# Turning the score maxima of an attention layer: four products with the identity on TensorE, or a split on GpSimd and squares of 32 turned on VectorE

## The chip, the cores and the metric

The kernel runs on one core of a Trainium2 chip. The metric is the device time of one launch in microseconds (us). TensorE (PE in the profile) multiplies matrices, VectorE (DVE) and ScalarE (ACT) do elementwise work, GpSimd (POOL) is a third elementwise engine, and SyncE (SP) issues the transfers. Each engine takes its instructions in the order in which the program lists them, and an instruction that waits holds up everything behind it on its engine.

## The reference

One layer of a hybrid transformer: 2048 rows of width 1024, a context of 256 rows, a bidirectional retention with 4 heads, attention with 8 query heads on 2 key heads of width 64, and an MLP with squared ReLU. The change lies in the attention:

```
def _dense_attention(q, k, v):
    s = jnp.einsum('bqkgd,bskd->bkgqs', q, k).astype(jnp.float32) * ATT_SCALE
    p = jax.nn.softmax(s, axis=-1).astype(v.dtype)
    return jnp.einsum('bkgqs,bskd->bqkgd', p, v)
...
    k_all = jnp.concatenate([k_ctx, k_lat], axis=1)
    v_all = jnp.concatenate([v_ctx, v_lat], axis=1)
```

Every query sees all 2304 keys. The softmax needs a shift near the greatest score of each query, or its exponentials overflow.

## The kernel before

**Groups.** The 2048 queries are 16 tiles of 128 rows; a tile with one of the two key heads is a group, so there are 32 groups, numbered 0 to 31, of 4 heads x 128 queries. The 2304 keys are 18 tiles of 128. A group goes through two passes over them.

**First pass: maxima.** `piece` (L177, L181) multiplies the queries of one head with 512 keys into one of two PSUM banks called `mp`; `maximum` (L190) reduces that bank on VectorE into a column of `nm`. There are 18 such pairs for a group. `least` (L196) then reduces the 20 columns to the negated maximum of each query and head, and writes it twice, into columns 64 and 96 of a tile `mt` of 128x4x128 that is zero elsewhere and holds a constant in column 80.

**The turn.** The maxima lie down the partitions, one for each query, and the second pass wants them along the free dimension. `turn` (L201) transposes `mt` by four products with the identity on TensorE into an `mp` bank. `rows` (L204, ScalarE) copies rows 64 to 127 of that bank, divided by `ROW` = 8192, as float16 into `qr[64:, 1]`. `rows2` (L208, VectorE) writes the remainder of that rounding into rows 96 to 127.

**Second pass: scores.** `scores` makes a score tile of 128 keys x 512 (4 heads x 128 queries) with two products into one of two banks `st`: L214 with `qr[:, 0]`, L215 with `qr[:, 1]`, whose lower rows meet the rows of `unit` in `ks2` (`ROW` in its rows 0, 16 and 32) and so subtract the maximum inside the product. `exp` (L220, ScalarE) turns `st` into `p`; `cast` (L224, ScalarE) makes the float16 part `phi`; `low` makes the remainder `plo`, on GpSimd for five of nine pairs of key tiles (L231) and on VectorE for the others (L233); `values` (L247, L249) multiplies both parts with the values.

**Order.** All engines' orders are written out by hand: `on(k, phase, ...)` puts a call into step k, and the phases of a step run in a fixed list. Group n begins its first pass at step 18n and its second at step 18n + 22, so the first pass of one group lies beside the second of the one before. In the same steps run the retention (products `okw`, L1633; decays `oqf` and `oqb`, L1657; the normalisation of its output, whose root L1561 and factor `mr` L1695 on GpSimd feed four ScalarE instructions L1701), the output projection (L1837 to L1839) and, in the later groups, differences of `h` (L1929) and their float16 parts (L72, L73). Before the attention come the input products, after it the MLP (from about 1475 us).

Of the kernel before, what the change touches and what calls it, by code (L numbers as in the profile page):

```python
# [11 lines left out]
F32 = mybir.dt.float32  # L12
F32R = mybir.dt.float32r
F16 = mybir.dt.float16
BF16 = mybir.dt.bfloat16
I32 = mybir.dt.int32
AF = mybir.ActivationFunctionType
ALU = mybir.AluOpType
AX = mybir.AxisListType
# [3 lines left out]
P = 128  # L23
# [6 lines left out]
NK = NT + NC  # L30
H = 4
CH = 128
HD = 64
# [3 lines left out]
PSHIFT = 8  # L37

ROW = 8192.0
# [17 lines left out]
def layer_kernel(ctx: ExitStack, tc: tile.TileContext, a: dict, out: bass.AP):  # L57
    nc = tc.nc
# [5 lines left out]
    ident = const.tile([P, P], F32, name="ident")  # L64
# [70 lines left out]
    kp = keep.enter_context(tc.tile_pool(name="kp", bufs=1, reuse_waits="tile"))  # L135
# [6 lines left out]
    early = kp.tile([P, NK * (VW + 1)], F32, name="early", tag="wv")  # L142
# [6 lines left out]
    class Group:  # L149
# [7 lines left out]
        def load(self):  # L157
            pool, tag = (mq, "mb") if self.n % 4 < 2 else (qp, "qr")
            self.qr = pool.tile([P, 2, 4, P], F16, name="qr", tag=tag, bufs=2)
            q = self.qr.rearrange("p x (j e) t -> p x j e t", e=2)  # L160
            for e in range(2):
                src = aq_d[self.t][64 * e : 64 * e + 64, :, 2 * self.g : 2 * self.g + 2]
                nc.sync.dma_start(q[:64, :, :, e], src)
                nc.sync.dma_start(q[64:, 0, :, e], src[:, 0])

        def minima(self, pool):
            if pool is None:
# [21 lines left out]
                src, dst = m.rearrange("p (e k) -> p e k", e=2), self.nm[:, h, :, 4]  # L189
            nc.vector.tensor_reduce(dst, src, axis=AX.X, op=ALU.max, negate=True)  # L190

        def least(self, mt):
            self.mt = mt
            nm = self.nm.rearrange("p a b c -> p (a b) c")
            for c in (64, 96):
                nc.vector.tensor_reduce(mt[:, :, c], nm, axis=AX.X, op=ALU.min)  # L196

        def turn(self, pool=None, tag="mp"):
            self.m = (pool or psS).tile([P, 4, P], F32, name="mp", tag=tag)
            for h in range(4):  # L200
                nc.tensor.transpose(self.m[:, h], self.mt[:, h], ident)  # L201

        def rows(self):
            nc.scalar.activation(self.qr[64:, 1], self.m[64:], AF.Copy, scale=1 / ROW)  # L204

        def rows2(self):
            lo = self.qr[96:, 1]
            nc.vector.scalar_tensor_tensor(lo, self.m[96:], 1 / ROW, lo, op0=ALU.mult, op1=ALU.subtract)  # L208

        def scores(self, kt):  # L210
            ps = self.s[kt] = psS.tile([P, 512], F32, name="st", tag="st")
# [62 lines left out]
    with ExitStack() as st, tc.manual_schedule():  # L274
# [3 lines left out]
        wp = st.enter_context(tc.tile_pool(name="wp", bufs=12, reuse_waits="tile"))  # L278
        sg = st.enter_context(tc.tile_pool(name="sg", bufs=3, reuse_waits="tile"))
        op = st.enter_context(tc.tile_pool(name="op", bufs=2, reuse_waits="tile"))  # L280
# [4 lines left out]
        psO = st.enter_context(tc.tile_pool(name="psO", bufs=5, space=PSUM, reuse_waits="tile"))  # L285
# [25 lines left out]
        def do(s, part, fn, *args):  # L311
            steps.setdefault((s, part), []).append((fn, args))
# [897 lines left out]
        for (g, col), w in weights.items():  # L1210
            s = first[g, col]
# [3 lines left out]
            for j in range(w.n):  # L1215
                f, h = s - 5 + j, s - 3 + j if j < 2 else s - 1
                if (g, col) == (0, C_AQ):
                    f, h = s - 7 + j, s - 4 + j
                if (g, col) == (1, C_RQ):
                    f, h = s - 9 + j, (s - 6, s - 5, s - 2, s - 2)[j]  # L1220
                f, h = f - early_by, h - early_by
# [3 lines left out]
        for n, (col, s) in enumerate(((C_RK, 5), (C_AKV, 6), (C_AQ, 12), (C_RQ, 16), (C_RV, 18), (C_RG, 26))):  # L1225
            w = weights[0, col]
# [47 lines left out]
        s = first[1, C_RG]  # L1274
# [18 lines left out]
            do(s + 7 + i, "vec", next_g.maximum, i)  # L1293

        def first_mt():
            one_g.mt0 = wp.tile([P, 4, P], F32, name="mt", tag="w")
            nc.gpsimd.memset(one_g.mt0, 0.0)
            nc.gpsimd.memset(one_g.mt0[:, :, 80], PSHIFT * math.log(2.0) * HD**0.5)

        do(s + 4, "pool", first_mt)  # L1300
        do(s + 7, "vec", lambda: one_g.least(one_g.mt0))
        do(s + 8, "turn", one_g.turn, psO, "pso")
        do(s + 9, "turned", one_g.rows)
        do(s + 9, "low", one_g.rows2)

        def start():

# [217 lines left out]
    for g in range(2):  # L1525
        nc.sync.dma_start(ks2[:64, g], ks[:64, g])
        nc.sync.dma_start(ks2[64:, g], a["unit"])
    mts = [vp.tile([P, 4, P], F32, name=f"mt{i}") for i in range(2)]
    for mt in mts:
        nc.gpsimd.memset(mt, 0.0)  # L1530

        nc.gpsimd.memset(mt[:, :, 80], PSHIFT * math.log(2.0) * HD**0.5)

    def bank(i, shape=(P, 4, P)):
        return psX.tile(list(shape), F32, name=f"bank{i}", tag=f"bank{i}")
# [3 lines left out]
    def on(k, phase, fn, *args):  # L1539
        events.setdefault((k, phase), []).append((fn, args))  # L1540
# [28 lines left out]
    def attention():  # L1569
        for n, g in enumerate(groups):  # L1570
            k = NK * n
            if n > 0:
                if n > 1:
                    on(k - 14, "dma", g.load)
                    on(k - 1, "late", g.minima, sm)
                for i in range(AHEAD1 if n == 1 else 0, NK):
                    on(k + i, "piece", g.piece, i)
                    on(k + i + 1, "maximum", g.maximum, i)
                on(k + NK, "chain", g.least, mts[n % 2])
                on(k + NK + 1, "piece", g.turn)  # L1580
                on(k + NK + 2, "cast", g.rows)
                on(k + NK + 3, "early", g.rows2)
            k += LAG
            for i in range(NK):
                on(k + i, "scores", g.scores, i)
                on(k + i + 1, "exp", g.exp, i)
            for j in range(NK // 2):
                on(k + 2 * j + 3, "cast", g.cast, j)
                if j in POOL_PAIRS:
                    on(k + 2 * j + 4, "low", g.low, j)  # L1590
                else:
                    for i in range(2):
                        on(k + 2 * j + 4 + i, "low", g.low, j, i)
                on(k + 2 * j + 7, "values", g.values, j)
            k += NK + 6
            on(k, "cast", g.evacuate)
            on(k + 1, "chain", g.invert)
            on(k + 1, "late", g.combine, ats)
        return NK * len(groups) + LAG + 9
# [826 lines left out]
def _constants():  # L2426
    f = np.float32
    t = np.arange(SEQ, dtype=f)

    def freqs(n):  # L2430
        return (np.float32(10000.0) ** (-np.arange(n, dtype=f) / f(n))).astype(f)

    ang = (t[:, None] * freqs(64)).astype(f)
    c, s = np.cos(ang).astype(f), np.sin(ang).astype(f)
    ret = np.stack([np.concatenate([c, c], 1), np.concatenate([-s, s], 1)], 1)
    row = np.repeat(np.arange(SEQ // 64, dtype=f), 64)
    col = np.tile(np.arange(64, dtype=f), SEQ // 64)
    af = freqs(16)
    ang = np.concatenate([row[:, None] * af, col[:, None] * af], 1).astype(f)
    c, s = np.cos(ang).astype(f), np.sin(ang).astype(f)  # L2440
    att = np.stack([np.concatenate([c, c], 1), np.concatenate([-s, s], 1)], 1)
    j, i = np.meshgrid(np.arange(P), np.arange(P), indexing="ij")
    one = np.ones((P, P))
    rel = np.stack([np.maximum(i - j, 0), np.maximum(j - i, 0), one * (i + 1), one * (P - i)], 1).astype(f)
    pos = np.stack([P - 1 - np.arange(P), np.arange(P)], 1).astype(f)
    unit = np.zeros((64, NK * P), np.float16)
    unit[[0, 16, 32]] = ROW
    return {"ret_cs": ret, "att_cs": att, "rel": rel, "pos": pos, "unit": unit}


# [33 lines left out]
```

## Time and profile before

| | |
|---|---|
| median of 3 runs | 2664.66 us (2662.99 to 2667.97) |
| the profiled execution | 2665.0 us, span of its instructions 2663.2 us |
| busy: PE, DVE, ACT, POOL | 98%, 76%, 57%, 65% of the span |
| granted TensorE clock | 0.997 of full speed |
| first and last transpose of a `turn` on TensorE | 589.9 and 1443.0 us |

A row of the timeline gives start, duration, engine, line, operation, result and operands, and in brackets the idle time before it with what ended it. Rows of the groups end with the count, the busy time in us, the mean duration in ns, and the idle time before. TensorE overlaps its products, so the time that one occupies is read from start to start. Engine spans on POOL are rough.

### The profile page before, as it was taken

Reading aid. Unit: us, or ns where it says so; the run is one execution under the profiler, and the core shown is the slowest. Engines: PE = TensorE matmul, PEld = TensorE weight load, DVE = VectorE, ACT = ScalarE, POOL = GpSimd, SP = SyncE. Lnnn points to the kernel's source line nnn. Section 1 sums busy time; section 2 is a strip of 40 time slices with the busy share of each in tenths; the row PEclk is TensorE's granted clock in tenths of the full one; section 3 lists DMA queues with packets and bytes.
Section 4 is the critical chain, followed back from the end, with each engine's and each line's share of the span. In section 5 each row is a group of like instructions: output and inputs, shape, how many; then the busy total and the mean of one; then the engine's idle time right before and its main releaser. Section 6 shows DMA issues by size and latency. Waiting matters only on the chain.

```text
span 2663.2 us, 45648 instructions
## 1 busy us (share of the span) xinstructions
PE 2615.4 (98%) x16745; PEld 1466.2 (55%) x16745; DVE 2028.8 (76%) x3035; ACT 1526.2 (57%) x2576; POOL 1741.0 (65%) x1355
## 2 busy tenths in 40 slices
PE   8999999998999999999999999999999999999998
PEld 5875555545666666666666444444444444444443
DVE  5778798667888888888887597888886656656686
ACT  3856343426877788888888476666665322222243
POOL 3635566545666668787887696677663666666686
PEclk9999999999999999999999999999999999999999
DMA  6776899736112123233422664677684757475453
GB/s 230 272 247 208 305 331 322 261 113 214 48 55 70 55 79 100 90 82 89 125 76 78 247 180 143 229 233 235 206 302 141 282 182 281 170 292 170 163 187 114
DMA packets 324713, 479.78 MB, mean 180 GB/s; under 512 B 82036, under 2 KB 191876, under 8 KB 320008
## 3 DMA queue, kind: packets, MB, share of 16 engines
q1 hardware_dynamic: 324472, 476.84, 54.1%
q8 instruction: 132, 2.16, 0.3%
q14 instruction: 93, 0.76, 0.1%
q10 hardware_dynamic: 16, 0.01, 0.0%
HBM read 319.79 MB, written 156.38 MB: 179 GB/s over the span
## 4 chain that ended last, share of the span: by engine, by line
PE 71%; ACT 3%; DVE 1%; DMA 1%; issue 0%; POOL 0%; SPq 0%; DVEq 0%; POOLq 0%; ACTq 0%
PE pd L2296 7%; PE pd L2297 7%; PE pd L2295 7%; PE pu L2069 7%; PE pu L2068 7%; PE pu L2070 7%; PE o L249 4%; PE st L214 4%; PE st L215 4%; PE mp L177 3%; PE o L247 2%; PE bank L1839 2%; PE bank L1837 2%; PE bank L1838 2%; ACT p L220 1%; ACT phi L224 1%
## 5 line engine op out<-in xcount | busy, mean ns | idle before, releaser
L190 DVE TENSOR_REDUCE nm<-mp 128x1 f32<-128x512 f32 x558 | 380.7, 686 | 116.7 <-PE mp L177 110.1
L231 POOL TENSOR_TENSOR plo<-p,phi 128x1024 f16<-128x1024 f32 x160 | 349.7, 2187 | 142.9 <-ACT phi L224 128.5
L220 ACT ACTIVATE p<-st 128x512 f32<-128x512 f32 x576 | 342.1, 601 | 157.7 <-PE st L215 157.1
L2068 PE MATMUL pu<-hf,w1f 128*128 128x512 f16 x896 | 339.6, 379 | 0.0
L2069 PE MATMUL pu<-hf,w1f 128*128 128x512 f16 x896 | 339.6, 379 | 0.0
L2070 PE MATMUL pu<-hf,w1f 128*128 128x512 f16 x896 | 339.6, 379 | 0.0
L2295 PE MATMUL pd<-w,uf 128*128 128x512 f16 x896 | 339.6, 379 | 0.0
L2296 PE MATMUL pd<-w,uf 128*128 128x512 f16 x896 | 339.6, 379 | 0.0
L2297 PE MATMUL pd<-w,uf 128*128 128x512 f16 x896 | 339.6, 379 | 0.0
L2315 POOL TENSOR_TENSOR y<-y,d 128x512 f32<-128x512 f32 x128 | 210.5, 1647 | 145.2 <-ACT uf L2284 98.9
L224 ACT ACTIVATE phi<-p 128x1024 f16<-128x1024 f32 x288 | 305.2, 1060 | 0.0
L233 DVE TENSOR_TENSOR plo<-p,phi 128x512 f16<-128x512 f32 x256 | 231.0, 904 | 21.5 <-ACT phi L224 9.1
L247 PE MATMUL o<-wv,plo 128*128 128x65 f16 x2304 | 230.5, 193 | 0.0
L249 PE MATMUL o<-wv,phi 128*128 128x129 f16 x2176 | 228.9, 220 | 0.0
L214 PE MATMUL st<-qr,ks 128*128 128x512 f16 x576 | 218.3, 379 | 6.5 <-ACT p L220 4.9
L247 PEld LDWEIGHTS <-plo 128*128 128x128 f16 x2304 | 205.4, 98 | 27.7 <-issue 1.9
L215 PE MATMUL st<-qr,ks 128*128 128x512 f16 x576 | 218.5, 379 | 0.0
L2307 DVE SCALAR_TENSOR_TENSOR y<-pd,scy,y 128x512 f32<-128x512 f32 x160 | 116.9, 747 | 132.3 <-PE pd L2297 131.0
L2080 DVE TENSOR_TENSOR r<-pu,r 128x512 f32<-128x512 f32 x224 | 149.8, 684 | 84.4 <-PE pu L2070 60.9
L1195 PE MATMUL pso<-wf,h_l 128*128 128x512 f16 (+1 forms) x576 | 208.2, 361 | 0.0
L1197 PE MATMUL pso<-wf,h_l 128*128 128x512 f16 (+1 forms) x576 | 208.1, 361 | 0.0
L1196 PE MATMUL pso<-wf,h_l 128*128 128x512 f16 (+1 forms) x576 | 208.1, 361 | 0.0
(389 smaller groups left out, 6131.9 us busy)
## 6 DMA issues: line engine op xcount, KB each, us to landing
wm<-in_w_ff SPq DMA_DIRECT2D x64, 512.0 KB, 7.4
u<-r SPq DMA_DIRECT2D x128, 256.0 KB, 4.2
ur<-u SPq DMA_DIRECT2D x128, 256.0 KB, 6.1
y<-x SPq DMA_DIRECT2D x64, 512.0 KB, 6.0
wf<-w2f SPq DMA_DIRECT2D x112, 256.0 KB, 2.9
w<-wf SPq DMA_DIRECT2D x28, 1024.0 KB, 10.1
w1r<-in_w_ff SPq DMA_DIRECT2D x48, 512.0 KB, 5.1
x<-y SPq DMA_DIRECT2D x48, 512.0 KB, 2.6
```

Of the source, the lines that this page charges most:

```text
L190: nc.vector.tensor_reduce(dst, src, axis=AX.X, op=ALU.max, negate=True)
L220: nc.scalar.activation(self.p[kt // 2][:, kt % 2], self.s.pop(kt), AF.Exp, scale=HD**-0.5)
L224: nc.scalar.activation(hi, self.p[j], AF.Copy)
L231: nc.gpsimd.tensor_tensor(lo, p, hi, op=ALU.subtract)
L247: mm(o[:, : HD + 1], lo[:, i, c], v[:, : HD + 1], start=False, stop=False)
L249: mm(o, hi[:, i, c], v[:, :VW], start=False, stop=last)
L2068: mm(pu[hf, i], whi, hi, start=k == 0, stop=False)
L2069: mm(pu[hf, i], whi, lo, start=False, stop=False)
L2070: mm(pu[hf, i], wlo, hi, start=False, stop=k == 3)
L2295: mm(ps, u[:, 0, b], w[:, b, 0], start=b == 0, stop=False)
L2296: mm(ps, u[:, 0, b], w[:, b, 1], start=False, stop=False)
L2297: mm(ps, u[:, 1, b], w[:, b, 0], start=False, stop=b == 3)
```

## The change

`least` reduces `nm` once, into a small tile `m4` of 128x4. A new step `parts` makes the float16 value of `m4 / ROW` and its remainder on GpSimd, with three instructions, into columns 0 and 1 of an `mt` that is now 128x4x32 in float16 (the constant is in column 16). `turn` is four VectorE transposes, one for each 32 queries; each takes 32 partitions x 4 x 32 elements and writes them, turned in squares of 32, straight into `qr[64:96, 1]`. `rows` and `rows2` are gone. `load` fetches the query rows into both halves of `qr[64:]` so that rows 96 to 127 hold finite values, and `unit` has `ROW` in rows 0, 1 and 16.

```
-                nc.sync.dma_start(q[64:, 0, :, e], src[:, 0])
+                nc.sync.dma_start(q[64:, :, :, e], src)
...
-        def least(self, mt):
+        def least(self, pool):
+            self.m4 = pool.tile([P, 4], F32, name="m4", tag="m4")
+            nc.vector.tensor_reduce(self.m4, self.nm.rearrange("p a b c -> p (a b) c"), axis=AX.X, op=ALU.min)
+
+        def parts(self, mt):
             self.mt = mt
-            nm = self.nm.rearrange("p a b c -> p (a b) c")
-            for c in (64, 96):
-                nc.vector.tensor_reduce(mt[:, :, c], nm, axis=AX.X, op=ALU.min)
-
-        def turn(self, pool=None, tag="mp"):
-            self.m = (pool or psS).tile([P, 4, P], F32, name="mp", tag=tag)
-            for h in range(4):
-                nc.tensor.transpose(self.m[:, h], self.mt[:, h], ident)
-
-        def rows(self):
-            nc.scalar.activation(self.qr[64:, 1], self.m[64:], AF.Copy, scale=1 / ROW)
-
-        def rows2(self):
-            lo = self.qr[96:, 1]
-            nc.vector.scalar_tensor_tensor(lo, self.m[96:], 1 / ROW, lo, op0=ALU.mult, op1=ALU.subtract)
+            nc.gpsimd.tensor_scalar_mul(mt[:, :, 0], self.m4, 1 / ROW)
+            nc.gpsimd.tensor_scalar_mul(self.m4, self.m4, 1 / ROW)
+            nc.gpsimd.tensor_tensor(mt[:, :, 1], self.m4, mt[:, :, 0], op=ALU.subtract)
+
+        def turn(self):
+            for i in range(0, P, 32):
+                nc.vector.transpose(self.qr[64:96, 1, :, i : i + 32], self.mt[i : i + 32])
...
-    mts = [vp.tile([P, 4, P], F32, name=f"mt{i}") for i in range(2)]
+    mts = [vp.tile([P, 4, 32], F16, name=f"mt{i}") for i in range(2)]
...
-                on(k + NK, "chain", g.least, mts[n % 2])
-                on(k + NK + 1, "piece", g.turn)
-                on(k + NK + 2, "cast", g.rows)
-                on(k + NK + 3, "early", g.rows2)
+                on(k + NK, "chain", g.least, qp)
+                on(k + NK, "late", g.parts, mts[n % 2])
+                on(k + NK + 2, "chain", g.turn)
...
-    unit[[0, 16, 32]] = ROW
+    unit[[0, 1, 16]] = ROW
```

Group 0, whose first pass lies beside the input products, is changed in the same way.

On GpSimd at the turn of group 16, before (`hp` and `hs` are the differences of `h` and their parts, `cy_gn` the root of the retention's normalisation, `plo` the low parts of the group before):

```order
L231 TENSOR_TENSOR plo<-p_13384,phi 128x1024
L1560 TENSOR_SCALAR cv_gn<-mv,gns 128x4
L1693 TENSOR_SCALAR mr<-mv 128x4
L1561 TENSOR_TENSOR cy_gn<-cv_gn,half 128x4
L73 TENSOR_TENSOR hp<-hb,hp 128x512
L1695 TENSOR_TENSOR mr<-mr,cy_gn 128x4
L1929 TENSOR_TENSOR hs<-hb,hs 128x512
L231 TENSOR_TENSOR plo<-p_13484,phi 128x1024
```

and the same place now (lines are those of the changed kernel, 5 to 7 lower):

```order
L227 TENSOR_TENSOR plo<-p_13384,phi 128x1024
L1554 TENSOR_SCALAR cv_gn<-mv,gns 128x4
L1686 TENSOR_SCALAR mr<-mv 128x4
L1555 TENSOR_TENSOR cy_gn<-cv_gn,half 128x4
L198 TENSOR_SCALAR mt_6725<-m_13528 128x4
L199 TENSOR_SCALAR m_13528<-m_13528 128x4
L200 TENSOR_TENSOR mt_6725<-m_13528,mt_6725 128x4
L73 TENSOR_TENSOR hp<-hb,hp 128x512
L1688 TENSOR_TENSOR mr<-mr,cy_gn 128x4
L1922 TENSOR_TENSOR hs<-hb,hs 128x512
L227 TENSOR_TENSOR plo<-p_13484,phi 128x1024
```

The three instructions of `parts` stand between the root and the factor `mr`, ahead of the part `hp`.

On VectorE at the same turn, before (`nm<-mp` are the maxima, here first those of the ending group and then those of the next):

```order
L190 TENSOR_REDUCE nm<-mp 128x2
L233 TENSOR_TENSOR plo<-p_13434,phi 128x512
L196 TENSOR_REDUCE mt_6725<-nm 128x4 x2
L190 TENSOR_REDUCE nm<-mp 128x1
L233 TENSOR_TENSOR plo<-p_13434,phi 128x512
L190 TENSOR_REDUCE nm<-mp 128x1 x2
L208 SCALAR_TENSOR_TENSOR qr<-mp,qr 32x512
L190 TENSOR_REDUCE nm<-mp 128x1 x3
```

and now:

```order
L190 TENSOR_REDUCE nm<-mp 128x2
L229 TENSOR_TENSOR plo<-p_13434,phi 128x512
L194 TENSOR_REDUCE m_13528<-nm 128x4
L190 TENSOR_REDUCE nm<-mp 128x1
L229 TENSOR_TENSOR plo<-p_13434,phi 128x512
L190 TENSOR_REDUCE nm<-mp 128x1
L204 STREAM_TRANSPOSE qr<-mt_6725 32x4x32 x4
L190 TENSOR_REDUCE nm<-mp 128x1 x4
```

The four transposes stand one maximum earlier than `rows2` did, and wait for GpSimd instead of ScalarE. On TensorE only the four products L201 of each group leave the order; on ScalarE only `rows`.

More of the change, by code (lines that the diff above doesn't have):

```diff
@@ L1295, in first_mt @@
         def first_mt():
-            one_g.mt0 = wp.tile([P, 4, P], F32, name="mt", tag="w")
+            one_g.mt0 = wp.tile([P, 8, P], F16, name="mt", tag="w")[:, :4, :32]
             nc.gpsimd.memset(one_g.mt0, 0.0)
-            nc.gpsimd.memset(one_g.mt0[:, :, 80], PSHIFT * math.log(2.0) * HD**0.5)
+            nc.gpsimd.memset(one_g.mt0[:, :, 16], PSHIFT * math.log(2.0) * HD**0.5 / ROW)
         do(s + 4, "pool", first_mt)
[L1301 to L1304, printed above, removed]
+        do(s + 7, "vec", one_g.least, kp)
+        do(s + 7, "pool", lambda: one_g.parts(one_g.mt0))
+        do(s + 8, "low", one_g.turn)
         def start():
@@ L1527, in layer_kernel @@
         nc.sync.dma_start(ks2[64:, g], a["unit"])
-    mts = [vp.tile([P, 4, P], F32, name=f"mt{i}") for i in range(2)]
+    mts = [vp.tile([P, 4, 32], F16, name=f"mt{i}") for i in range(2)]
     for mt in mts:
         nc.gpsimd.memset(mt, 0.0)
-        nc.gpsimd.memset(mt[:, :, 80], PSHIFT * math.log(2.0) * HD**0.5)
+        nc.gpsimd.memset(mt[:, :, 16], PSHIFT * math.log(2.0) * HD**0.5 / ROW)
     def bank(i, shape=(P, 4, P)):
```

## The prediction

> **What bounds the kernel now.** I read the page first, then the busy time in stretches, then who makes TensorE wait.
>
> ```profile
> span 2663.2 us, 45648 instructions
> PE 2615.4 (98%) x16745; PEld 1466.2 (55%) x16745; DVE 2028.8 (76%) x3035; ACT 1526.2 (57%) x2576; POOL 1741.0 (65%) x1355
> 860.00:960.00 100.00, 99.08 (x942) 65.53 (x940) 81.54 (x150) 79.40 (x131) 65.71 (x51) 1.00 0.19 62
> 1900.00:2100.00 200.00, 200.00 (x929) 90.65 (x927) 143.34 (x175) 115.44 (x190) 94.97 (x62) 1.00 0.73 243
> PE st L214 <- ACT p L220: 4.9, 16, 0.3
> PE mp L201 <- DVE mt L196: 0.7, 1, 0.7
> ```
>
> TensorE is busy 98% of the span, 99.08 of 100 us in a stretch of the attention and all of 200 us in the MLP behind it. In the attention VectorE has 18 us in 100 to spare, ScalarE 21, GpSimd 34. Of the waits of TensorE (the last two rows; us in all, times, longest) few belong to this place. So a product that leaves TensorE's order in the attention moves the end by the time it occupied, unless another engine is late at that spot.
>
> **What leaves TensorE.** What a turn occupies is read from start to start, in group 14 and, where it came late, in group 17:
>
> ```profile
> 982.29 0.38 PE L215 MATMUL st<-qr,ks 128*128 128x512 f16 x1
> 982.51 0.60 PE L201 MATMUL mp<-ident,mt 128*128 128x128 f32 x4
> 982.95 0.38 PE L177 MATMUL mp<-ks,qr 128*128 128x512 f16 x1
> ...
> 1062.68 0.38 PE L215 MATMUL st<-qr,ks 128*128 128x512 f16 x1
> 1063.07 0.63 PE L201 MATMUL mp<-ident,mt 128*128 128x128 f32 x4
> 1063.57 0.38 PE L177 MATMUL mp<-ks,qr 128*128 128x512 f16 x1
> ```
>
> and the same instructions as one group (count, shortest, median and longest ns, first and last start):
>
> ```profile
> L201 PE MATMUL mp<-ident,mt x128: 272/273/301, 589.9 to 1443.0; 128*128 128x128 f32 x128
> ```
>
> Four transposes take 982.95 - 982.51 = 0.44 us; 32 groups make 14.1 us. In group 17, and in 21, 25 and 29, which repeat its pattern, L215 to L177 is 0.89 us instead of 0.66: 4 x 0.23 = 0.9 more. Group 2's turn waits 0.7 for `mt` (above). Together 14.1 + 0.9 + 0.7 = 15.7 us. The row of L201 has 273 ns for one transpose, which is its passage and not its place. [...] The trace has that duration, but the next product begins 0.11 us for each transpose later, and that decides.
>
> **What leaves and joins VectorE and ScalarE.**
>
> ```profile
> L208 DVE SCALAR_TENSOR_TENSOR qr<-mp,qr 32x512 f16<-32x512 f32 x32 | 22.3, 697 | 9.9 <-ACT qr L204 9.0
> L196 DVE TENSOR_REDUCE mt<-nm 128x4 f32<-128x20 f32 x62 | 7.5, 160 | 0.0
> L1111 DVE TENSOR_SCALAR early<-early 128x128 f32<-128x128 f32 x4 | 1.1, 279 | 0.0
> L204 ACT ACTIVATE qr<-mp 64x512 f16<-64x512 f32 x32 | 19.0, 592 | 0.8
> 1010.27 0.68 DVE L1874 TENSOR_TENSOR u<-bank,a 128x512 f32<-128x512 f32 x1
> 1011.24 0.38 PE L177 MATMUL mp<-ks,qr 128*128 128x512 f16 x1
> 1014.52 0.38 PE L177 MATMUL mp<-ks,qr 128*128 128x512 f16 x1
> ```
>
> VectorE loses 0.70 us of `rows2` and the second reduce (7.5 us over 62, about 0.1). No turn in squares is in the trace. From below, one cannot cost less than the reduce of 4 columns, 0.16; from above I take `rows2`, 0.70, with the same 32 partitions and four times the elements. An operation with the same 128 elements a lane is L1111, 0.279, and I take that: four make 1.1 us, 0.3 more than what goes. In group 15 the squares stand behind L1874, which ends at 1010.27 + 0.68 = 1010.95. ScalarE loses 0.59 a group, which only makes `exp` earlier. The `mp` bank that a turn held until `rows2` is free for the maxima; TensorE hardly waits for one now, so nothing is counted. The loads carry twice the bytes into rows 64 to 127, in the same number of transfers, 14 steps ahead of their use; DMA is at 0.19 of its time in the stretch above: nothing, and if one came late, the turn would wait for it on VectorE.
>
> **What joins GpSimd, and who is queued behind.** Three instructions of 128x4 a group.
>
> ```profile
> L1693 POOL TENSOR_SCALAR mr<-mv 128x4 f32<-128x4 f32 x15 | 3.0, 197 | 0.0
> L1695 POOL TENSOR_TENSOR mr<-mr,cy_gn 128x4 f32<-128x4 f32 x15 | 5.1, 338 | 0.5
> L1561 POOL TENSOR_TENSOR cy_gn<-cv_gn,half 128x4 f32<-128x4 f32 x15 | 15.8, 1053 | 0.0
> 1035.46 1.02 POOL L1561 TENSOR_TENSOR cy_gn<-cv_gn,half 128x4 f32<-128x4 f32 x1
> 1036.46 1.58 POOL L73 TENSOR_TENSOR hp<-hb,hp 128x512 f16<-128x512 f32 x1
> 1038.00 0.20 POOL L1695 TENSOR_TENSOR mr<-mr,cy_gn 128x4 f32<-128x4 f32 x1
> 1038.23 0.88 ACT L1701 ACTIVATE oo<-oo,mr,cy_gn 128x128 f32<-128x128 f32 x2
> 1037.46 0.69 DVE L190 TENSOR_REDUCE nm<-mp 128x1 f32<-128x512 f32 x1 [0.44 <-PE mp L177]
> 1043.24 0.60 ACT L220 ACTIVATE p<-st 128x512 f32<-128x512 f32 x1
> 1044.53 0.38 PE L214 MATMUL st<-qr,ks 128*128 128x512 f16 x1
> ```
>
> Two scalings at 0.197 and a subtraction at 0.338 are 0.74 us; no lower than 3 x 0.197 = 0.6, no higher than three of the costliest row of that size, 3.2. In group 16 they end at 1036.48 + 0.74 = 1037.2, and VectorE gets to its squares after the maximum that ends at 1038.15, less 0.44 since TensorE is early: it does not wait. But there GpSimd has no idle time, and `mr` moves from 1038.20 to about 1038.95. ScalarE's L1701 needs it, and has begun at 1038.23 straight after `mr`. It begins 0.45 (if `hp` runs in 1.26, as elsewhere) to 0.75 us later, and the `exp` behind it too, since ScalarE is busy up to 1043.84. The `st` bank of that `exp` is refilled at 1044.53: 0.69 to spare, less 0.44 by which TensorE is early. TensorE waits 0.2 to 0.5; I take 0.35 in groups 16, 20, 24 and 28, 1.4 us.
>
> ```profile
> 634.52 0.25 DVE L196 TENSOR_REDUCE mt<-wmx 128x4 f32<-128x20 f32 x2
> 633.95 1.54 POOL L1633 TENSOR_TENSOR okw<-ork,kd 128x512 f32<-128x512 f32 x1 [2.77 <-PE st L215]
> 641.46 2.13 POOL L231 TENSOR_TENSOR plo<-p,phi 128x1024 f16<-128x1024 f32 x1
> 644.62 0.19 PE L247 MATMUL o<-wv,plo 128*128 128x65 f16 x1
> ...
> 1006.81 0.24 DVE L196 TENSOR_REDUCE mt<-nm 128x4 f32<-128x20 f32 x2
> 1005.06 1.27 POOL L1657 TENSOR_TENSOR oqf<-oqt,tf 128x512 f32<-128x512 f32 x1
> 1008.95 2.13 POOL L231 TENSOR_TENSOR plo<-p,phi 128x1024 f16<-128x1024 f32 x1 [0.93 <-DVE plo L233]
> 1015.82 0.19 PE L247 MATMUL o<-wv,plo 128*128 128x65 f16 x1
> ```
>
> In group 1 `parts` waits for the maxima at 634.68 and `okw` for `parts`, until 635.4 instead of 633.95. GpSimd has no gap up to the `plo` of 641.46, which then ends near 645.05; TensorE used it at 644.62. That group's 0.44 us is not gained and 0.45 is lost: 0.9. In the other odd groups it is the same wait with more cover. In group 15 `oqf` stands until 1007.0 + 0.74 = 1007.7 instead of 1005.06, and eats the 0.93 us of idle time before the next `plo`, which begins about 2.64 - 0.93 = 1.7 later and ends at 1012.8; TensorE needs it at 1015.82. Nothing is counted; without that cover it would cost up to 1.7 us a time.
>
> Sum: 15.7 - 1.4 - 0.9 = 13.4 us, all of it ahead of the MLP, whose first transfers start from tiles that the attention gives back and so move with it. The profiled execution took 2665.0, 1.8 more than its span and 0.3 more than the median; from the median, 2664.66 - 13.4 = 2651.3 us.
>
> **Rivals.** A difference under about 0.2% (5.3 us) cannot be told from none here.
>
> First, GpSimd is later than I count. At 1.5 us for `parts`, twice my count and under half of the upper bound, groups 16, 20, 24, 28 lose 0.76 more each and group 1 as well, 3.8 us: 2655; at 2 us, 2658. Behind it can stand contention:
>
> ```profile
> 1060.07 2.13 POOL L231 TENSOR_TENSOR plo<-p,phi 128x1024 f16<-128x1024 f32 x1
> 1060.20 2.55 DVE L233 TENSOR_TENSOR plo<-p,phi 128x512 f16<-128x512 f32 x1
> ```
>
> VectorE's subtraction took 2.55 us here beside one of GpSimd's, where L1874 of the same size took 0.68. [...] 16 in 100.
>
> Second, ScalarE sets the pace and the 0.44 us come back as longer waits at the place of the row `PE st L214 <- ACT p L220`, once in two groups: 13 us given back, 2663. For it: 16 waits of 0.3. Against it: ScalarE itself waits for TensorE in every group and gets 0.59 lighter. 8 in 100.
>
> Third, slower: the squares are dear. Behind them on VectorE are two maxima that give back the `mp` banks. In group 15 the product at 1014.52 needs the bank of the one at 1011.24, whose maximum takes 0.7 and, with 0.3 for the hand-over, can begin at 1013.5 at the latest, 2.5 us after 1010.95. Each us of turns beyond 2.5 stops TensorE for as long; from 2.5 + 0.44 = 2.94 us, 0.74 for a square, the change loses. At 0.9, a little over the upper bound, it is 32 x (3.6 - 2.94) = 21 us: 2686. For it: four starts instead of one, and no row. Against it: no row of 128 elements a lane is near 0.74 without contention. 10 in 100.
>
> **The numbers.** The forecast, 2651.3, has 66 in 100; its own bounds are 2646 (neither loss, 2649, and over half of the 4.9 us of waits for `exp` gone too) and 2656 (squares at their upper bound stop TensorE for 0.3 us in 16 odd groups, 4.8 us). With the first rival it reaches 2660, and 2646 to 2660 holds about 8 in 10. Faster: 0.66 + 0.16 = 0.82; same 0.08; slower 0.10.
>
> **What would show it.** Right: no L201 rows, L215 to the next product 0.22 us in group 14, TensorE's busy time down by some 13 us, transposes of 0.2 to 0.35 us without idle time before them, `parts` near 0.75, and new waits of TensorE for `p` in groups 16, 20, 24, 28 and for `plo` in group 1. Wrong: VectorE idle before the transposes with GpSimd as the cause, TensorE waiting for `nm` in every group, or waits for `p` of 0.9 us in every second one.

## The result, and the profile after

The changed kernel took 2656.33 us (median of 7, 2653.78 to 2660.59) beside 2665.25 us (2662.99 to 2668.75) of the kernel before: a ratio of 0.9964, interval 0.9955 to 0.9973. That is 8.9 us less, where 13.4 were forecast; the time lies in the predicted range, 5.0 us above the forecast. The profiled execution took 2656.33 us. Its page and the same stretch of the attention as before:

```profile
span 2654.5 us, 45435 instructions
PE 2601.0 (98%) x16617; PEld 1450.9 (55%) x16617; DVE 2049.4 (77%) x3099; ACT 1504.7 (57%) x2544; POOL 1761.7 (66%) x1451
```

```profile
860.00:960.00 100.00, 99.09 (x947) 65.39 (x946) 84.82 (x160) 78.15 (x130) 68.53 (x64) 1.00 0.22 67
```

TensorE has 128 products and 14.4 us of busy time less. VectorE has 3.3 us more in 100, ScalarE 1.3 less, GpSimd 2.8 more, and TensorE is as full as before. The steps that joined, as groups of the timeline between 600 and 1460 us, where 31 of the 32 turns lie (count, busy time, mean ns, idle time before them):

```profile
L204 DVE STREAM_TRANSPOSE qr<-mt 32x128 f16<-32x128 f16 x124 | 37.6, 303 | 2.5
L198 POOL TENSOR_SCALAR mt<-m 128x4 f16<-128x4 f32 x31 | 10.6, 341 | 28.2 <-DVE m L194 26.6
L199 POOL TENSOR_SCALAR m<-m 128x4 f32<-128x4 f32 x31 | 6.8, 221 | 2.6
L200 POOL TENSOR_TENSOR mt<-m,mt 128x4 f16<-128x4 f32 x31 | 6.8, 218 | 2.6
```

A square takes 0.303 us, `parts` 0.341 + 0.221 + 0.218 = 0.78; with two gaps of 0.08 between its instructions it holds GpSimd for 0.94 from start to end. VectorE hardly waits ahead of the squares (2.5 us over 124); GpSimd does wait for the maxima ahead of `parts`, 26.6 us in all. The timeline of the places that the prediction spoke of, group 14 on TensorE and group 16 on GpSimd and ScalarE:

```profile
982.34 0.38 PE L211 MATMUL st<-qr,ks 128*128 128x512 f16 x1
982.56 0.38 PE L177 MATMUL mp<-ks,qr 128*128 128x512 f16 x1
...
1035.73 0.56 POOL L198 TENSOR_SCALAR mt<-m 128x4 f16<-128x4 f32 x1
...
1036.83 1.16 POOL L73 TENSOR_TENSOR hp<-hb,hp 128x512 f16<-128x512 f32 x1
1037.95 0.20 POOL L1688 TENSOR_TENSOR mr<-mr,cy_gn 128x4 f32<-128x4 f32 x1
1038.18 0.88 ACT L1694 ACTIVATE oo<-oo,mr,cy_gn 128x128 f32<-128x128 f32 x2 [1.47 <-POOL mr L1688]
```

From L211 to L177 it is 0.22 us, where L215 to L177 was 0.66. In group 16 ScalarE now sits idle 1.47 us for `mr`. TensorE is 1.3 us earlier behind that turn, so `mr`, at 1037.95 beside 1038.00, is late by almost as much relative to it. Two things nearly cancel here: from the start of `parts` to that of `hp` it is 1.10 us where 0.74 was counted, and `hp` takes 1.16 instead of 1.58.

Without the transposes TensorE has the same 16617 products in the same order in both kernels, so each can be compared with itself. The start of one product in the changed kernel minus its start in the kernel before, worked out from the two traces (us; negative is earlier; the third column is a second profile of the changed kernel, taken with the last experiments):

| at (time of before) | changed | changed, again |
|---|---|---|
| 500, input products | +1.4 | +1.1 |
| 595, behind group 0's turn | +0.6 | +1.0 |
| 640, in group 1 | -0.9 | +0.7 |
| 690, behind group 3's turn | +4.4 | +5.9 |
| 1030, ahead of group 16's turn | -0.8 | +0.7 |
| 1445, end of the attention | -7.0 | -5.5 |
| end | -8.4 | -5.0 |

So the gain is in place from group 4 on: 11.4 us both times. The first groups of the attention lose 3.8 and 4.9 us (595 to 690) where the forecast had a gain of 1.1. What stands ahead of 595 and behind 1445 differs between two profiles of the same kernel by as much as 1.9 us.

The figures from 595 to 690 us hold an element of chance. In some stretches of 3.41 us the granted TensorE clock is at 0.50, which costs an estimated 1.7 us at most each, half of their length, and where they fall differed between the two profiles of the changed kernel. The kernel before has one of them there, at 631 to 635 us, the changed kernel one, at 650 to 653, and the changed kernel again two, at 617 to 621 and 652 to 655. The part of the loss that comes back the same lies between 640 and 655 us: 5.3 and 5.4 us, the stretch at 650 or 652 included.

Where the start loses, the timeline of before

```profile
642.78 1.36 DVE L233 TENSOR_TENSOR plo<-p,phi 128x512 f16<-128x512 f32 x1
644.66 0.68 DVE L233 TENSOR_TENSOR plo<-p,phi 128x512 f16<-128x512 f32 x1
644.74 2.59 POOL L231 TENSOR_TENSOR plo<-p,phi 128x1024 f16<-128x1024 f32 x1 [1.16 <-ACT phi L224]
662.32 0.88 ACT L1701 ACTIVATE oo<-oo,mr,cy_gn 128x128 f32<-128x128 f32 x2
```

and that of the changed kernel:

```profile
635.21 0.24 POOL L198 TENSOR_SCALAR mt<-m 128x4 f16<-128x4 f32 x1 [3.56 <-DVE m L194]
635.98 1.04 POOL L1626 TENSOR_TENSOR okw<-ork,kd 128x512 f32<-128x512 f32 x1
642.98 4.66 POOL L227 TENSOR_TENSOR plo<-p,phi 128x1024 f16<-128x1024 f32 x2
643.05 2.60 DVE L229 TENSOR_TENSOR plo<-p,phi 128x512 f16<-128x512 f32 x1
646.17 2.01 DVE L229 TENSOR_TENSOR plo<-p,phi 128x512 f16<-128x512 f32 x1
648.84 0.38 PE L177 MATMUL mp<-ks,qr 128*128 128x512 f16 x1 [1.72 <-DVE nm L190]
...
667.07 0.20 POOL L1688 TENSOR_TENSOR mr<-mr,cy_gn 128x4 f32<-128x4 f32 x1
667.31 0.88 ACT L1694 ACTIVATE oo<-oo,mr,cy_gn 128x128 f32<-128x128 f32 x2 [1.16 <-POOL mr L1688]
```

`parts` wait for the maxima until 635.21, and `okw` behind them begins at 635.98 instead of 633.95. Two `plo` behind that come back to back, the first 1.5 us later than before, and VectorE's two subtractions beside them take 2.60 and 2.01 us instead of 1.36 and 0.68. The maximum behind the second comes late, TensorE waits 1.72 us for it, and then runs at half its clock. (A row of windows gives the stretch, its length, the busy time and count of TensorE, weight loads, VectorE, ScalarE and GpSimd, then the granted clock, the DMA share and GB/s. The first of the three is an earlier stretch, with the end of a wait of 3.11 us in it, that was not followed by half clock.)

```profile
629.45:632.86 3.41, 1.67 (x24) 1.53 (x24) 2.32 (x6) 0.00 (x0) 1.04 (x1) 1.00 0.64 243
646.52:649.93 3.41, 1.42 (x9) 0.67 (x7) 3.41 (x5) 1.65 (x3) 1.12 (x1) 1.00 0.94 286
649.93:653.34 3.41, 3.41 (x26) 2.80 (x25) 1.25 (x3) 1.09 (x3) 0.41 (x1) 0.50 1.01 356
```

In group 2 `mr` stands behind `parts`, ScalarE is idle for 1.16 us, and TensorE waits for `p`. Three rows of TensorE's list of waits over the whole span (us in all, times, longest):

```profile
PE st L210 <- ACT p L216: 6.3, 18, 0.6
PE mp L177 <- DVE nm L190: 2.4, 3, 1.7
PE o L243 <- POOL plo L227: 0.2, 1, 0.2
```

### The profile page after: what moved, and what is told of

The parts are those of the page before. It is cut to its first block, busy times and chain, and to the rows that moved or that the text cites. A ratio compares the mean times of both kernels' runs of the same rounds, so it can differ in the third digit from the quotient of the medians.

```text
span 2654.5 us, 45435 instructions
## 1 busy us (share of the span) xinstructions
PE 2601.0 (98%) x16617; PEld 1450.9 (55%) x16617; DVE 2049.4 (77%) x3099; ACT 1504.7 (57%) x2544; POOL 1761.7 (66%) x1451
## 3 DMA queue, kind: packets, MB, share of 16 engines
q8 instruction: 130, 2.13, 0.3%
## 4 chain that ended last, share of the span: by engine, by line
PE 69%; ACT 3%; POOL 2%; DVE 1%; DMA 1%; issue 0%; SPq 0%; POOLq 0%; DVEq 0%; ACTq 0%
PE pd L2290 7%; PE pd L2289 7%; PE pd L2288 7%; PE pu L2063 7%; PE pu L2061 7%; PE pu L2062 7%; PE st L210 4%; PE o L245 4%; PE st L211 4%; PE mp L177 3%; PE o L243 2%; PE bank L1832 2%; PE bank L1830 2%; PE bank L1831 2%; ACT p L216 1%; ACT phi L220 1%
## 5 line engine op out<-in xcount | busy, mean ns | idle before, releaser
L229 DVE TENSOR_TENSOR plo<-p,phi 128x512 f16<-128x512 f32 x256 | 240.1, 939 | 21.8 <-ACT phi L220 9.4
L211 PE MATMUL st<-qr,ks 128*128 128x512 f16 x576 | 218.5, 379 | 0.0
```

## The experiments

Each ran beside the kernel before on the same chip. The third and fourth asked what the 0.44 us and the squares are worth; the others asked what the start lost. Each run left one profile, so how many stretches of half clock it met is chance as well: between 595 and 690 us `parts` on VectorE in group 1 has three such stretches, the relieved kernel none, the loaded kernel and the first run of the best order one, the others two.

**Parts on VectorE, in group 1 alone and in all groups.**

```
-            nc.gpsimd.tensor_scalar_mul(mt[:, :, 0], self.m4, 1 / ROW)
...
+            eng = nc.vector if self.n == 1 else nc.gpsimd
+            eng.tensor_scalar_mul(mt[:, :, 0], self.m4, 1 / ROW)
...
```

For all groups the line is `eng = nc.vector`.

> The changed kernel, with the three instructions of parts on VectorE instead of GpSimd for group 1 alone. Theory A (some 6 us of the expected gain were lost once, in group 1, where GpSimd's okw waits behind parts for the maxima and the low parts behind it then block VectorE's subtractions): about 6 us faster than the changed kernel, 2649 to 2652, with TensorE's waits for okw, plo and nm between 635 and 675 us gone and the two subtractions that took 2.6 and 2.0 us at 643 to 648 near 0.7 to 1.4. Theory B (the start of the attention varies by itself from one program to the next, and parts has no share in it): within 2 us of the changed kernel, 2654 to 2658.

> The changed kernel, with parts on VectorE for all groups, so GpSimd has no share in the turn. Theory A with its second half (in groups 16, 20, 24 and 28 parts delays the factor mr, ScalarE starts later and TensorE waits 0.39 us each): 6 us for group 1 and 1.6 us for those four, about 7.5 us faster than the changed kernel, 2648 to 2650, and no TensorE waits for p at 1039, 1146, 1253 and 1360 us. Rival (VectorE is near its limit, 0.5 us more of it for each group costs as much on TensorE): 2656 to 2665, with TensorE waiting for nm in most groups.

Group 1 alone: 2657.78 us (2656.51 to 2661.31), ratio 0.9964, interval 0.9951 to 0.9977, no better than the change. From 595 to 690 it loses 3.8 us too. All groups: 2695.43 us, ratio 1.0106, interval 1.0088 to 1.0124, slower than the kernel before. The timeline of group 1 in the first (the last two rows are the two subtractions that meet a `plo` in the change), and TensorE's longest list of waits in the second:

```profile
635.83 0.81 DVE L199 TENSOR_SCALAR mt<-m 128x4 f16<-128x4 f32 x1
636.67 1.18 DVE L200 TENSOR_SCALAR m<-m 128x4 f32<-128x4 f32 x1
637.89 1.21 DVE L201 TENSOR_TENSOR mt<-m,mt 128x4 f16<-128x4 f32 x1
...
647.18 0.68 DVE L230 TENSOR_TENSOR plo<-p,phi 128x512 f16<-128x512 f32 x1
...
648.38 0.68 DVE L230 TENSOR_TENSOR plo<-p,phi 128x512 f16<-128x512 f32 x1
```

```profile
PE mp L177 <- DVE nm L190: 34.8, 31, 2.8
```

The three small instructions took 3.2 us on VectorE beside GpSimd's work, where they take 0.78 on GpSimd. The time of the first run could not decide on the queue of GpSimd, since it put as much on VectorE as it took from there. Its trace says more: the two subtractions take 0.68 us each, no wait at that place is over 0.5 us, and only 0.7 us is lost from 640 to 655, where the change lost 5.3. The loss lies ahead of that: TensorE waits 0.7 and 0.9 us for maxima at 640 to 642, behind the late `parts`, and half clock falls at 617 to 621 and 631 to 638 us. The second run was 30 us or more slower than either theory gave. The rival's sign, waits for `nm` in most groups, is there 31 times: VectorE has no room for `parts`.

**The products back, idle.** Four products of the identity with itself stand in groups 1 to 31 where the transposes stood; nothing reads them.

```
+        def idle_turn(self):
+            d = psS.tile([P, 4, P], F32, name="mp", tag="mp")
+            for h in range(4):
+                nc.tensor.transpose(d[:, h], ident, ident)
...
+                on(k + NK + 1, "piece", g.idle_turn)
```

> The changed kernel, with four products of the identity with itself added on TensorE where the turn stood, in groups 1 to 31; they write an mp bank that nothing reads, so nothing waits for them. If a turn is worth the time from its start to the next product, 0.44 us, this is 31 x 0.44 = 13.6 us slower than the changed kernel, about 2670. If it were worth the passage in the record, 1.1 us for four, it is 34 us slower, 2690. If the change gained by taking the waits for ScalarE and VectorE away rather than by the products, it is within 3 us of the changed kernel.

2668.18 us (2665 to 2673), ratio 1.0007, interval 0.9997 to 1.0016: 11.9 us above the median of the changed kernel, or 10.5 if each is set against the kernel before that ran beside it. From 690 to 1445 us it loses 0.6 us where the change gains 11.4, so four products cost 0.43 in each of these 28 turns. The whole gain there is TensorE's slots; at the 273 ns of the row of L201, 31 turns would have been 34 us.

**Every square twice.**

```
-            for i in range(0, P, 32):
+            for i in 2 * list(range(0, P, 32)):
```

> The changed kernel, with each of the four squares' transposes on VectorE done twice: 2.5 us in place of 1.25 for a group. By the prediction's working VectorE may stay on them for 2.5 us before TensorE misses a bank: within 4 us of the changed kernel, 2654 to 2660. If VectorE's time is worth its price on TensorE already: 32 x 1.25 = 40 us slower, 2696.

2707.42 us (2701 to 2710), ratio 1.0146, interval 1.0128 to 1.0164: 51 us above the changed kernel, where the prediction's own rule (2.5 us of squares are free, each us beyond costs one) left 0.15 us a turn, 5 us in all. Its timeline in an odd group and TensorE's longest list of waits:

```profile
800.87 2.65 DVE L204 STREAM_TRANSPOSE qr<-mt 32x128 f16<-32x128 f16 x8
808.60 2.13 POOL L227 TENSOR_TENSOR plo<-p,phi 128x1024 f16<-128x1024 f32 x1 [0.67 <-ACT phi L220]
809.01 2.27 DVE L229 TENSOR_TENSOR plo<-p,phi 128x512 f16<-128x512 f32 x1
```

```profile
PE mp L177 <- DVE nm L190: 22.7, 30, 1.7
```

The squares end at 803.5 and stop nobody by themselves. VectorE then works without a pause, meets a `plo` at 809.01, and its subtraction takes 2.27 us. TensorE waits 1.5 us for the maximum behind it, and the granted clock is at half from about 813 to 816. The offset grows by 3.7 us there, and 690 to 1445 us lose 34 us instead of gaining 11. Six stretches of half clock hold an estimated 10 of these 45 us, at up to 1.7 each.

**Two moves on GpSimd.** In even groups the factor `mr` (which the step `link` emits) ahead of `parts`; in group 1 the one `okw` ahead of them; and both.

```
+                if n % 2 == 0:
+                    on(k + NK, "late", link)
                 on(k + NK, "late", g.parts, mts[n % 2])
...
-            on(k - 2, "late", weigh, d, c)
+            on(k - 2, "pe" if (d, c) == (1, 0) else "late", weigh, d, c)
```

> One line is added: in even groups the last link of the retention's root, the factor `mr` on GpSimd, is put ahead of the three instructions of `parts` instead of behind them. Theory: in groups 2, 16, 20, 24 and 28 ScalarE's normalisation waits for `mr` behind `parts` (1.16 us idle in group 2), the exponentials behind it come late and TensorE waits for `p`: 0.73 + 0.69 + 0.65 us in group 2, where 0.45 stood before, and 0.26 + 0.13 in each of the four others. With `mr` first, 1.6 + 1.6 us come back: 2653 us, and no row of ScalarE idle for `mr`. Rival: these waits come from something else (TensorE being 0.44 us early in every group): 2656 us and the same rows.

> One `okw` of the retention, the one that stands behind group 1's `parts` on GpSimd, is put ahead of them. Theory: the start of the attention loses 4.2 us against the kernel before because `parts` wait there for the maxima until 635.2 us, `okw`, `oqf`, `oqb` and two `plo` come 1.4 to 2.0 us later behind them, and the later `plo` fall on two of VectorE's subtractions (2.60 and 2.01 us instead of 1.36 and 0.68), so that the maxima, and TensorE for 1.88 us, wait. With `okw` first GpSimd is where it was in the kernel before: the two subtractions are near 1.4 and 0.7 us again, the wait is gone, and 2 to 4 us come back: 2652 to 2654 us. Rival: the start is bound by VectorE, and the 0.55 us by which four squares are longer than the row operation set the loss: no more than 0.7 us comes back, 2655.6 us or over.

> Both moves on GpSimd together: `mr` ahead of `parts` in even groups, and the one `okw` ahead of group 1's `parts`. If both theories hold the gains add: 3.2 + 2 to 4 us less than the changed kernel, 2649 to 2651 us, which is what the prediction gave or a little under. If only the first holds 2653, if neither 2656 us.

`mr` first: 2657.39 us, ratio 0.997, interval 0.996 to 0.998. `okw` first: 2655.11 us (2649.82 to 2656.21), ratio 0.9958, interval 0.9945 to 0.997. Both: 2654.6 us, ratio 0.9966, interval 0.9952 to 0.998. All three missed the time of their theory: 2653 was expected for the first, 2652 to 2654 for the second, 2649 to 2651 for both. From 595 to 690 us they lose 4.2, 2.4 and 1.3 us. With `mr` first ScalarE's idle time in group 2 falls from 1.16 to 0.36 us and the waits for `p` with it, but nothing is gained. The timeline of the kernel with both moves shows why:

```profile
663.46 4.22 POOL L227 TENSOR_TENSOR plo<-p,phi 128x1024 f16<-128x1024 f32 x2
663.55 1.26 DVE L204 STREAM_TRANSPOSE qr<-mt 32x128 f16<-32x128 f16 x4 [0.43 <-POOL mt L200]
667.63 1.83 DVE L229 TENSOR_TENSOR plo<-p,phi 128x512 f16<-128x512 f32 x1 [0.29 <-ACT phi L220]
669.98 2.29 DVE L229 TENSOR_TENSOR plo<-p,phi 128x512 f16<-128x512 f32 x1
```

The squares now wait 0.43 us for `parts`, the exponentials come earlier, and both subtractions fall beside a `plo`: 1.83 and 2.29 us, where the change had 1.27 and 0.68. TensorE waits 2.0 us for `nm` instead, here and with `mr` first alone. So for group 2 that theory falls: the wait for `mr` was real, but taking it away put a wait for a maximum in its place.

**VectorE relieved, VectorE loaded.** The first takes 0.60 us from VectorE behind group 1's squares, on top of `okw` first: one update of the retention's state is copied by ScalarE and leaves out the decayed state. The second adds 0.68 us to the kernel before, a maximum reduced twice; it was meant to stand behind group 1's `rows2`, and in the trace it stands just ahead of it.

```
-            if old is None:
+            if old is None or (d, c, hs) == (1, 0, (0, 1)):
                 nc.scalar.activation(t[:, hs[0] : hs[0] + 2], ps[:, hs[0] : hs[0] + 2], AF.Copy)
```

```
+            for _ in range(2 if (self.n, i) == (2, 2) else 1):
+                nc.vector.tensor_reduce(dst, src, axis=AX.X, op=ALU.max, negate=True)
```

> The kernel of the run with `okw` first, with one thing taken from VectorE behind group 1's squares: of the state update `sb` of the last step ahead of the attention's regular part, two of four instructions (0.60 us, about what four squares take more than the row operation) become a copy on ScalarE, so this one update leaves out the decayed state. Theory now: group 1 has lost its 3 us because VectorE comes 0.2 to 0.5 us later to its second subtraction of a pair, so that GpSimd's `plo` begins first and the subtraction takes 2.4 us instead of 0.7; TensorE then waits 1.8 us for a maximum and its granted clock is at one half for 3.4 us behind it. With VectorE 0.6 us earlier the subtraction begins ahead of `plo`: near 0.7 us, no wait over 0.6 us near 648, 1.7 to 3.4 us less than with `okw` first: 2651.7 to 2653.4 us. Rival: the loss is TensorE's or GpSimd's and not VectorE's place: 2655 us, the wait stays.

> The kernel before, with one maximum of group 2 (its third) reduced twice, right behind group 1's `rows2` on VectorE: 0.68 us more there, once in the whole kernel, a little more than the 0.55 us by which the squares are longer. Theory: this alone moves the second subtraction behind GpSimd's `plo`, which makes it 1.5 us or more longer, TensorE waits for a maximum near 646 us, and 2 to 4 us are lost from 634 to 672 us: 2667 to 2669 us beside 2665. Rival: VectorE has 0.68 us to spare there: 2665 to 2665.7 us.

Relieved: 2652.15 us (2651.1 to 2653.9), ratio 0.9954, interval 0.9941 to 0.9966, and 595 to 690 us lose nothing (-0.1). Loaded: 2665.32 us, ratio 1.0, interval 0.9991 to 1.0009: no loss. On the timelines, `okw` first, relieved, then loaded:

```profile
633.09 1.04 POOL L1626 TENSOR_TENSOR okw<-ork,kd 128x512 f32<-128x512 f32 x1 [2.96 <-DMA ork<-rk]
633.16 1.52 DVE L229 TENSOR_TENSOR plo<-p,phi 128x512 f16<-128x512 f32 x1
...
644.82 2.43 DVE L229 TENSOR_TENSOR plo<-p,phi 128x512 f16<-128x512 f32 x1
```

```profile
632.10 0.68 DVE L229 TENSOR_TENSOR plo<-p,phi 128x512 f16<-128x512 f32 x1
632.27 1.41 POOL L1626 TENSOR_TENSOR okw<-ork,kd 128x512 f32<-128x512 f32 x1 [2.89 <-DMA ork<-rk]
...
640.43 5.12 POOL L227 TENSOR_TENSOR plo<-p,phi 128x1024 f16<-128x1024 f32 x2
641.70 1.86 DVE L229 TENSOR_TENSOR plo<-p,phi 128x512 f16<-128x512 f32 x1
```

```profile
643.47 0.68 DVE L234 TENSOR_TENSOR plo<-p,phi 128x512 f16<-128x512 f32 x1
644.67 0.68 DVE L234 TENSOR_TENSOR plo<-p,phi 128x512 f16<-128x512 f32 x1
```

The relieved kernel came in at the time that was expected, but its trace does not show that the relief did it. The subtraction at 641.70 still takes 1.86 us where some 0.7 was expected. GpSimd gives way too (5.12 us for two `plo`, where 2.13 each would make 4.26), and TensorE waits 1.7 us for `plo` but for no maximum. The two kernels part earlier, ahead of the squares. With `okw` first alone, `okw` began 0.07 us ahead of a subtraction at 633 us, which then took 1.52 us, and the next one 1.65. In the relieved kernel that subtraction began 0.17 us ahead of `okw`, and both took 0.68. This puts VectorE 1.8 us ahead, three times what the relief gives, before the relieved place is reached. Part of the rest is that the relieved kernel met no half clock from 595 to 690 us. What the relief alone is worth is not shown.

The loaded kernel was meant to lose 2 to 4 us and lost none. In the kernel before, the subtraction at 642.78 takes 1.36 us because a `plo` runs until 643.59. Loaded, it begins at 643.47, takes 0.68 and ends at 644.15, as before; the next one begins at 644.67 in place of 644.66. So VectorE had 0.68 us to spare there, and its extra 0.55 us alone are not the cause. That it takes them together with a GpSimd that comes without a gap fits the traces and was not tested by itself.

**The best order, and the change again.** `okw` first, and `mr` directly behind `parts` (the `link` one line lower), so that it is no longer behind `hp` in groups 16, 20, 24 and 28, while `parts` keep their place.

```
                 on(k + NK, "late", g.parts, mts[n % 2])
+                if n % 2 == 0:
+                    on(k + NK, "late", link)
```

> `okw` first as before, and in even groups the factor `mr` directly behind `parts`, so that in groups 16, 20, 24 and 28 it no longer stands behind a part `hp` of 1.3 to 1.6 us; `parts` themselves stay where the change put them. Theory: ScalarE's normalisation begins there as early as in the kernel before or earlier, the waits for `p` of 0.26 and 0.13 us in each of the four groups go, and since VectorE gets its squares no later, nothing takes their place: 1.6 us less than with `okw` first, 2653.5 us; this would be the best version so far. Rival: as with `mr` ahead of `parts`, waits for `nm` take their place: 2655 us.

> The changed kernel once more, for a second profile of the start of the attention. If the collision of group 1 (a subtraction of 2.0 us or more beside `plo`, TensorE waiting 1.9 us for a maximum near 647 us, half clock behind it) belongs to the kernel, it is there again and the offset grows by some 4 us from 590 to 685 us. If it is decided anew in each execution, by some tenths of a us, it may be missing, and the span is then 2 to 4 us shorter, at 2651 to 2652 us. Median 2656 us either way.

> The version with `okw` ahead of group 1's `parts` and `mr` directly behind `parts`, once more, beside the changed kernel on the same chip: if its two moves are worth what the traces say (0.7 to 1.6 us in the four groups, 0 to 3 at the start), it is 1 to 4 us below the changed kernel, 2652 to 2655 us; if the earlier difference was chance, the two agree within 1 us.

2652.34 us (2649.31 to 2654.89), and again 2651.52 us (2649.08 to 2655.36), ratios 0.9954 (0.9941 to 0.9966) and 0.995 (0.9937 to 0.9963). Beside the second stood the changed kernel on the same chip, 2656.65 us (2653.95 to 2659.73), ratio 0.9964 (0.9952 to 0.9976). So this order is 4 to 5 us below the changed kernel and 13 to 14 us below the kernel before, about what the change was forecast to give. The second profile of the changed kernel shows the same collision as the first,

```profile
644.56 2.61 DVE L229 TENSOR_TENSOR plo<-p,phi 128x512 f16<-128x512 f32 x1
647.70 2.01 DVE L229 TENSOR_TENSOR plo<-p,phi 128x512 f16<-128x512 f32 x1
```

and the best order (the second run) a milder one:

```profile
633.25 1.52 POOL L1628 TENSOR_TENSOR okw<-ork,kd 128x512 f32<-128x512 f32 x1 [2.78 <-DMA ork<-rk]
641.16 0.99 DVE L229 TENSOR_TENSOR plo<-p,phi 128x512 f16<-128x512 f32 x1
641.54 5.13 POOL L227 TENSOR_TENSOR plo<-p,phi 128x1024 f16<-128x1024 f32 x2
642.82 1.87 DVE L229 TENSOR_TENSOR plo<-p,phi 128x512 f16<-128x512 f32 x1
```

The two engines still meet, and both pay (0.99 and 1.87 us, and 5.13 for two `plo`), but TensorE waits for no maximum there, and for `plo` less than 0.5 us at a time. From 595 to 690 us it loses 0.3 and 0.0 us, against 3.8 and 4.9 of the change; from 690 to 1445 it gains 12.1 instead of 11.4. The 1.6 us of waits for `p` in the four groups are gone, but only 0.7 came back; a step of about 0.2 us at a product with `okw` in the group behind each of them took part of the rest.

`okw` first alone has the same program in group 1 as the best order, and its one profile has the collision (2.43 us, and TensorE waits 1.5). What differs is the order of two starts at 633 us, shown above. In the four other profiles with `okw` first the subtraction there took 0.68 us and `okw` paid (1.41 to 1.60 us), with starts between 0.02 us behind and 0.17 us ahead of it. So a tenth or two of a us seems to decide in each execution; with one profile a kernel it was not tried how often either comes.

Over all runs: the five profiles in which `parts` stand ahead of `okw` on GpSimd (the change twice, idle products, squares twice, `mr` first) all have a wait of 1.5 to 1.7 us for a maximum, ending at 648 to 650 us. Of the seven that have `okw` first or group 1's `parts` on VectorE, `okw` first has one there, `parts` on VectorE in all groups has one of 1.9 us at 641, and in the other five none between 636 and 650 us is over 0.9.

## Why the prediction was right and wrong

- **TensorE's slots: right.** 0.44 us start to start, not 273 ns of passage, is what a turn was worth. From group 4 on the offset falls by 0.44 us at every turn. The forecast for these 28 groups was 28 x 0.44 + 0.9 - 1.4 = 11.8 us; 11.4 came in two profiles, and giving the slots back cost 12.1 there. The late turns of groups 17, 21, 25 and 29 brought 0.2 each, as counted.
- **Price of a square and of `parts`: right.** 0.303 us for an estimated 0.279, 0.78 for 0.74. The sum left out the gaps between the instructions, which make it 0.94 of GpSimd's time. VectorE waited for `parts` 0.4 us once, in group 0, and otherwise at most 0.14.
- **`mr` behind `parts` in groups 16, 20, 24, 28: right.** The offset goes back by 0.26 + 0.13 us in each, 1.6 for 1.4; that the size fits is in part luck, since `parts` held GpSimd longer there than counted and `hp` was shorter. The same step failed to count group 2, where `mr` stands behind `parts` too: ScalarE idle 1.16 us, and TensorE's waits for `p` near 670 us 1.7 us where the kernel before had 0.3.
- **Group 1: the term that was mis-sized.** The step "`okw` waits behind `parts`, 0.9 us in all" had the queue right and the `plo` too: it was used at 645.16 where 645.05 was forecast. What it left out was who works beside the shifted `plo`: two subtractions that became 1.2 and 1.3 us longer, the maximum behind them, 1.7 us of waiting and a half clock. Groups 1 to 3, group 2's `mr` included, lost 3.8 and 4.9 us instead of gaining 1.1. These 4.9 to 6.0 us hold the whole shortfall of the forecast, 4.5 us of gain in the medians. How much of them is half clock is chance: the kernel before has a stretch of its own there.
- **The odd groups' `plo`: right.** No other wait for `plo` or `oqf` appears; loads and SP cost nothing that the waits show.
- **First rival.** It gave 2655 to 2658, and the time fell there, 0.3 us above the forecast's own upper bound of 2656. So it is this rival that keeps the time inside the stated range, and for half of its reason. Its first half, `parts` at 1.5 us, is wrong. Its second half, the subtractions beside GpSimd, is what happened, in one group: 2.60 and 2.01 us, where both took 0.68 with that group's `parts` on VectorE.
- **Second rival: wrong.** The waits for `p` at the middle of a pair stayed at 14 of 0.3 us between 690 and 1445 us.
- **Third rival: not entered, and wrong in its point of decision.** At 0.303 us a square the change was far from 0.74 on paper. Squares done twice, 2.65 us a turn, lost 41 us against the kernel before, where 2.94 us was the point of no gain. The cover of 2.5 us was read from two maxima behind the squares; the next subtraction, which had to be ahead of `plo`, was the nearer limit. (The 0.3 us for the hand-over in that working was an allowance that no row shows; in the rows a maximum ends at 648.79 and the product that waits for it begins at 648.84.) The right cover lies between 1.25 and 2.65 us; only these two points were tried.

## What to carry to other kernels

The slots taken from TensorE, 98% busy, paid 0.44 us in every turn from group 4 on, the size that is read from start to start. What such a change costs elsewhere has to be looked for where the regular pattern has not begun: here TensorE was busy for 25.34 of the 30 us from 620 to 650 us in the kernel before, beside 99.08 of 100 later, and a step that waited until 635.21 us at the head of GpSimd's queue moved `okw` behind it by 2.0 us and a `plo` onto other neighbours. So for each queue that a new waiting step joins, look which instructions behind it will run beside what, and put the step behind whatever is ready sooner: here two changes of order were together worth 5 us of 14.

## What the runs showed of the hardware that was not expected

- A wait of TensorE can cost more than itself, and whether it does is in part chance. Between 0.56 and 1.49 ms the granted clock is at 0.50 for stretches of 3.41 us, twice for two in a row (from 631 us with group 1's `parts` on VectorE, from 1473 us with `mr` first). In the one of the changed kernel at 650 us the two products of a score tile start 0.42 us apart (652.23 and 652.65), and 0.22 behind it (654.10 and 654.32); so a stretch costs an estimated 1.7 us at most. The same product L181 waits for a maximum in both kernels: 3.29 us until 630.76 in the kernel before, where half clock followed from 631.36, and 3.11 us until 631.19 in the changed kernel, where the clock stayed at 1.00 until 649.93. A wait of 1.72 us until 648.84 in the changed kernel was followed by the half clock at 649.93. So the length of the wait alone does not decide; what does was not shown.
- Where a subtraction of VectorE and a `plo` met in these rows, the order of their starts went with who took longer. In the kernel before VectorE's subtraction began 0.08 us ahead of `plo` and took 0.68, and `plo` took 2.59; in the changed kernel it began 0.07 us behind one and took 2.60.
- Three instructions of 128x4 elements took 3.2 us on VectorE where GpSimd was at work beside them (2.00 of 2 us from 636 to 638 us), and 0.78 on GpSimd itself.
- The squares of 32 were very even: 302 to 307 ns over the 128 of the changed kernel.
